# Query and gate projections a token chunk ahead of their cross-attention, with the second set held in an input buffer

## The chip, the cores and the metric

The program runs on one core of one Trainium2 chip. The metric is the device time of one execution in microseconds (us). A core has TensorE (PE in the profile, its weight loads PEld), VectorE (DVE), ScalarE (ACT), GpSimd (POOL) and SyncE (SP), which issues nearly all transfers here. Each engine works through its own list of instructions in a fixed order and stops at an instruction whose semaphores are not yet up.

## The reference, cut to what matters

```python
h = rmsnorm(x, pre_norm_w[i])                 # 4096 tokens x 1024
u = h @ w_in[i]
y_ssm  = mamba2_group(u[..., :SSM_IN], ...)                    # 512 columns
y_rwkv = rwkv7_group(u[..., SSM_IN:SSM_IN + RWKV_IN], ...)     # 256 columns
y_mem  = memory_xattn_group(u[..., SSM_IN + RWKV_IN:], mem_k, mem_v)   # 256 columns
y = jnp.concatenate([y_ssm, y_rwkv, y_mem], axis=-1)
x = x + rmsnorm(y @ w_out[i], post_norm_w[i])

def memory_xattn_group(u, mem_k, mem_v):      # 4 heads x 64, 256 memory tokens
    q = u[..., :XATTN_WIDTH].reshape(b, l, XATTN_HEADS, HEAD_DIM)
    g = u[..., XATTN_WIDTH:]
    s = jnp.einsum('blhd,bmhd->bhlm', q, mem_k) * (HEAD_DIM ** -0.5)
    p = jax.nn.softmax(s, axis=-1)
    o = jnp.einsum('bhlm,bmhd->blhd', p, mem_v).reshape(b, l, XATTN_WIDTH)
    return o * jax.nn.silu(g)
```

## The kernel before

The 4096 tokens are worked in 16 chunks of 256. Three phases follow one another: a (Mamba), b (RWKV) and c (cross-attention, output projection, norm and residual). The change touches phase c alone, which begins near 1587 us, while the last RWKV chunks are still being finished. Every float32 operand of a product is split into a high and a low part (`hh`/`hl`, `yh`/`ylo`, `phi`/`plo`, `wo0h`/`wo0l`), and a product is three matmuls: high by high, high by low, low by high.

For chunk i phase c has these streams:

- `load_hT(i)` (L112) fetches the normalised, transposed input of the chunk, `hh` and `hl`, 1 MB each, in two DMAs on SP. There are two buffers for it.
- `qg` (L1067) makes queries and gate. The 48 matmuls of `proj_cm` (L137, 128x256) for the queries go into one PSUM tile `pq`, the 48 for the gate into another, `pg`; both are `ps_pj` tiles, of which there are two in turn. `qs` is then split off `pq` by ACT and DVE (L1077, L1078), and the gate `sg` made by a tanh on ACT (L1084) and a product on DVE (L1085) that reads `pg` last.
- `units` does the four heads, named by a pair p and a side g: `score(p, g)` is 4 matmuls (L1110, L1111) into the PSUM tile `ps_g` or `ps_yo`, then a maximum (L1112), an exponential with its sum (L1115) and the division (L1119); `turn(p, g)` is 4 transposes (L1128) into `ps_tr` and their split into `phi` (ACT) and `plo` (DVE, L1132); `values(p)` is 8 matmuls (L1140) into a `ps_pj` tile, combined, gated and split into rows 6 and 7 of `yh`/`ylo`.
- `rest` loads the other rows of Y, which phases a and b have written (L1093).
- `outp(i)` (L1160) projects the two halves t=0 and t=1 of the chunk: 24 matmuls (L147, 128x512) into `ps_yd` and 24 into `ps_st`. Then the norm: ACT squares and sums both (L1172), POOL makes the factor in three small steps (L1174 to L1176), DVE scales both halves out of PSUM (`ot`, L1179), POOL adds the residual (L1180), SP stores (L1181). The next half's first `ps_yd` matmul waits for the first L1179, because there is one tile of each.

The loop at the end of phase c runs, for each i, `outp(i-1)`, `attn(i)` (that is `qg`, `rest`, `units`) and `load_hT(i+1)` beside one another. `weave` (L95) merges such streams by the weights written beside them, which fixes the order in which the instructions are written; a scheduler then fixes one list per engine. The transition is `start` (L1199): chunk 0's `qg`, memory keys and values, the load of chunk 1, the conversion of the first half of `w_out`, all woven with the end of the RWKV chain (`tail`; its steps on PE are L878, L885, L895, L912, L915, L946). The second half of `w_out` (`wo1`) is loaded later, through the two `xr` buffers (L1239).

Of the kernel before, what the change touches and what calls it, by code (L numbers as in the profile page):

```python
# [14 lines left out]
P = 128  # L15
# [12 lines left out]
def tile_hymba_trunk(  # L28
# [123 lines left out]
    def chain(*gens):  # L152
        for gen in gens:
            yield from gen
# [864 lines left out]
    def phase_c(b_tail, b_l, wqg, r14):  # L1019
# [41 lines left out]

        def attn(i, hT, Y):
            r = ahead if i == 1 else {}
            if i > 1:
                yield from qg(hT, r, 24)
            rest(i, Y)
            yield from units(Y, r)  # L1067

        def qg(hT, r, step):
            qs = [ca.tile([P, 2, NT], F32R, name=f"qs{h}", tag=f"qs{h}") for h in range(2)]  # L1070
            pq = ps_pj()
            for b_ in range(2):
                yield from proj_cm(blocks(wq)[b_], hT, pq[:, b_ * NT:(b_ + 1) * NT], step)
            pqv = pq.rearrange("p (b t) -> p b t", b=2)
            for h in range(2):
                hs, os_ = slice(h * 64, h * 64 + 64), slice((1 - h) * 64, (1 - h) * 64 + 64)
                s.copy(out=qs[h][hs], in_=pqv[hs])  # L1077
                v.tensor_tensor(out=qs[h][os_], in0=pqv[hs], in1=qs[h][hs].bitcast(F32), op=ALU.subtract)  # L1078
            pg = ps_pj()
            for b_ in range(2):  # L1080
                yield from proj_cm(blocks(wxg)[b_], hT, pg[:, b_ * NT:(b_ + 1) * NT], step)
            pgv = pg.rearrange("p (b t) -> p b t", b=2)
            sg = ca.tile([P, 2, NT], F32, name="sg", tag="sg")
            s.activation(out=sg, in_=pgv, func=AF.Tanh, scale=0.5)  # L1084
            v.scalar_tensor_tensor(out=sg, in0=sg, scalar=1.0, in1=pgv, op0=ALU.add, op1=ALU.mult)  # L1085
            r.update(qs=qs, sg=sg)

# [9 lines left out]
        def units(Y, r, tags=("g", "yo")):  # L1097
# [53 lines left out]

            for step in ((score, 0, 0), 1, (score, 0, 1), 1, (score, 1, 0), 3, (turn, 0, 0), 1, (turn, 0, 1), 4, (values, 0), 1,
                         (score, 1, 1), 1, (turn, 1, 0), 5, (turn, 1, 1), 4, (values, 1), 1):
                if isinstance(step, tuple):
                    step[0](*step[1:])
                else:
                    for _ in range(step):
                        yield

        def outp(i, Y):  # L1160
            for t in range(NPT):
                j = i * NPT + t
                xr = cw.tile([P, D], F32, name="xr", tag="xr", bufs=2)
                sy.dma_start(out=xr, in_=x2[j * P:(j + 1) * P, :])
                pos = [psum("yd", 1), psum("st", 1)]
                for n_ in range(2):
# [29 lines left out]
        late = ExitStack()  # L1196
        ahead = {}

        def start():  # L1199
            hT = new_hT()  # L1200
            yield from load_hT(0, hT)
            r = {}
            with right("cm") as cm:
                yield from chain2(memory(cm), qg(hT, r, 8))
            wr = ctx.enter_context(right("wr"))
            ws = late.enter_context(right("ws"))
            hT1 = new_hT()
            yield from load_hT(1, hT1)
            both = [units(Ys[0], r, None), chain(*(load_o(wr, ws, n_) for n_ in range(2)))]
            while both:  # L1210
                for gen in list(both):
                    if next(gen, gen) is gen:
                        both.remove(gen)
                    yield
            yield from qg(hT1, ahead, 8)
            rest(0, Ys[0], range(2))
# [30 lines left out]
        Ys.append(new_Y(cw))  # L1247
        hT = None
        for i in range(1, NS + 1):
# [3 lines left out]
            if i < NS:  # L1253
                streams.append((attn(i, hT, Ys[i % 2]), 28))
            if i + 1 < NS:
                hT = new_hT()
                streams.append((load_hT(i + 1, hT), 4))
            weave(*streams)
# [31 lines left out]
```

## Time and profile before

| what | value |
|---|---|
| time, median of 3 runs | 2271.78 us (2269.9 to 2273.0) |
| the profiled execution | 2275.23 us, its span 2273.5 us |
| granted TensorE clock over the span | 0.98 of full speed |
| PE busy | 2179.0 us (96%) |
| DVE, ACT, POOL busy | 1521.4, 1182.1, 709.0 us |
| DMA | 218.87 MB, mean 96 GB/s |

The span runs from the first to the last instruction on the core. PE busy counts overlapped matmuls once; a matmul's shown duration is longer than the distance to the next one, since they are pipelined. "Idle before <- X" names what ended an engine's wait.

### The profile page before, as it was taken

What the parts mean: (1) busy time and instruction counts of PE and PEld (TensorE: products, weight loads), DVE (VectorE), ACT (ScalarE), POOL (GpSimd) and SP (SyncE); (2) the same over time, 40 slices, a digit from 0 to 9 for tenths busy, and PEclk for the clock granted to TensorE, in tenths of its full rate; (3) what the DMA queues carried; (4) which work ended last, traced back from release to release, by engine and by line L of the source; (5) the groups of instructions that cost most, each with busy time, mean ns of one, the idle gap of its engine ahead of it and who ended that gap; (6) DMA issues with size and microseconds to landing.
All of it is one profiled execution on the core that took longest, in us unless ns stands there. A gap on an engine that the chain in (4) does not pass through costs nothing.

```text
span 2273.5 us, 51147 instructions
## 1 busy us (share of the span) xinstructions
PE 2179.0 (96%) x20705; PEld 1997.3 (88%) x20705; DVE 1521.4 (67%) x3442; ACT 1182.1 (52%) x2877; POOL 709.0 (31%) x1039
## 2 busy tenths in 40 slices
PE   4999999999999889999999999999899999999997
PEld 4999999999999788898989889888778888888885
DVE  5788878877878877667677777776644544545442
ACT  6555555545554565566666666676533433334331
POOL 1343434343433343333343333331122221222212
PEclk8999999999999999999999999998899999999999
DMA  6232223322233321111111111124333333333321
GB/s 200 88 139 91 94 94 113 121 94 94 93 139 105 116 83 39 67 57 48 43 44 63 61 48 44 44 90 163 121 135 130 125 121 144 113 115 125 121 70 56
DMA packets 83611, 218.87 MB, mean 96 GB/s; under 512 B 9191, under 2 KB 45486, under 8 KB 71086
## 3 DMA queue, kind: packets, MB, share of 16 engines
q1 hardware_dynamic: 82334, 215.59, 27.2%
q8 instruction: 163, 2.67, 0.5%
q14 instruction: 74, 0.61, 0.1%
q10 hardware_dynamic: 1040, 0.00, 0.0%
HBM read 152.00 MB, written 63.57 MB: 95 GB/s over the span
## 4 chain that ended last, share of the span: by engine, by line
PE 78%; DVE 8%; ACT 5%; DMA 4%; POOL 2%; issue 2%; POOLq 0%; SPq 0%; DVEq 0%; ACTq 0%
PE ps_pj L137 37%; PE ps_yd L147 8%; PE ps_pj L147 7%; PE ps_st L147 7%; DVE cc L296 3%; DMA R<-rowd 1%; PE ps_yo L878 1%; DMA w_st<-in_w_in_dram 1%; PE ps_yd L730 1%; PE ps_yd L425 1%; PE ps_tr L126 1%; ACT w_hi L78 1%; PE ps_yo L895 1%; PE ps_yo L885 1%; PE ps_st L730 1%
## 5 line engine op out<-in xcount | busy, mean ns | idle before, releaser
L137 PE MATMUL ps_pj<-hh,w_hi 128*128 128x256 f32 x2704 | 789.4, 292 | 7.2 <-ACT w_hi L78 5.4
L137 PE MATMUL ps_pj<-hh,w_lo 128*128 128x256 f32 x2704 | 778.6, 288 | 1.5 <-DVE w_lo L79 1.5
L137 PE MATMUL ps_pj<-hl,w_hi 128*128 128x256 f32 x2704 | 776.8, 287 | 0.0
L137 PEld LDWEIGHTS ps_pj<-hh,w_hi 128*128 128x128 f32 x2704 | 519.4, 192 | 18.8 <-issue 4.0
L137 PEld LDWEIGHTS ps_pj<-hh,w_lo 128*128 128x128 f32 x2704 | 519.1, 192 | 8.1 <-DVE w_lo L79 2.5
L137 PEld LDWEIGHTS ps_pj<-hl,w_hi 128*128 128x128 f32 x2704 | 519.7, 192 | 6.8
L296 DVE SCALAR_TENSOR_TENSOR cc<-ux,cwh,cc 128x256 f32<-128x256 f32 x384 | 220.0, 615 | 16.0 <-ACT cc L293 12.4
L147 PE MATMUL ps_pj<-w_hi,hh 128*128 128x260 f32 (+1 forms) x528 | 156.5, 297 | 22.4 <-DVE dtr L270 16.8
L147 PE MATMUL ps_pj<-w_hi,hl 128*128 128x260 f32 (+1 forms) x528 | 153.1, 290 | 0.0
L147 PE MATMUL ps_pj<-w_lo,hh 128*128 128x260 f32 (+1 forms) x528 | 152.5, 289 | 0.0
L147 PEld LDWEIGHTS ps_pj<-w_hi,hh 128*128 128x128 f32 x528 | 102.5, 194 | 25.1 <-issue 16.9
L147 PE MATMUL ps_yd<-wo0h,yh 128*128 128x512 f32 x256 | 103.9, 406 | 12.0 <-DVE ot L1179 12.0
L147 PE MATMUL ps_st<-wo1h,yh 128*128 128x512 f32 x256 | 103.8, 406 | 0.0
L147 PEld LDWEIGHTS ps_pj<-w_lo,hh 128*128 128x128 f32 x528 | 102.5, 194 | 0.3
L147 PEld LDWEIGHTS ps_pj<-w_hi,hl 128*128 128x128 f32 x528 | 102.4, 194 | 0.0
L147 PE MATMUL ps_yd<-wo0l,yh 128*128 128x512 f32 x256 | 102.3, 400 | 0.0
L147 PE MATMUL ps_yd<-wo0h,ylo 128*128 128x512 f32 x256 | 101.9, 398 | 0.0
L147 PE MATMUL ps_st<-wo1l,yh 128*128 128x512 f32 x256 | 101.7, 397 | 0.0
L147 PE MATMUL ps_st<-wo1h,ylo 128*128 128x512 f32 x256 | 100.8, 394 | 0.0
L299 ACT ACTIVATE th<-cc 128x512 f32<-128x512 f32 x64 | 40.4, 632 | 112.0 <-DVE cc L296 110.5
L1113 POOL TENSOR_SCALAR mx<-mx 128x2 f32<-128x2 f32 x64 | 14.6, 228 | 260.3 <-DVE mx L1112 238.1
L1180 POOL TENSOR_TENSOR xr<-ot,xr 128x512 f32<-128x512 f32 x64 | 84.7, 1347 | 32.7 <-DVE ot L1179 32.7
(443 smaller groups left out, 5086.0 us busy)
## 6 DMA issues: line engine op xcount, KB each, us to landing
hl<-hTd SPq DMA_DIRECT2D x32, 1024.0 KB
hh<-hTd SPq DMA_DIRECT2D x32, 1024.0 KB
xt<-in_x_dram SPq DMA_DIRECT2D x32, 512.0 KB
hTd<-hh SPq DMA_DIRECT2D x16, 1024.0 KB
hTd<-hl SPq DMA_DIRECT2D x16, 1024.0 KB
R<-rowd SPq DMA_DIRECT2D x32, 512.0 KB
xr<-in_x_dram SPq DMA_DIRECT2D x32, 512.0 KB
out_dram<-xr SPq DMA_DIRECT2D x32, 512.0 KB
```

The costliest lines, as they stand in the source:

```text
L78: s.activation(out=hi[:, ki, :], in_=st[:, k, 0:n], func=AF.Copy, scale=sc)
L126: te.transpose(pt[:, q * P:(q + 1) * P], src[:, k * P:(k + 1) * P], ident)
L137: te.matmul(outp, lhsT=a[:, k, :], rhs=b[:, k, :], start=(n == 0), stop=(n == 3 * KB - 1))
L147: te.matmul(outp, lhsT=a[:, k, tsl], rhs=b[:, k, 0:ncol], start=(n == 0), stop=(n == 3 * KB - 1))
L296: v.scalar_tensor_tensor(out=cc[:, b_, :], in0=ux[:, b_, j:j + NT], scalar=wj(j), in1=cc[:, b_, :], op0=ALU.mult, op1=ALU.add)
L299: s.activation(out=th, in_=cc, func=AF.Tanh)
L425: te.matmul(yd[hf * 64:hf * 64 + 64, h * 64:h * 64 + 64], lhsT=R[:, h, hf * 64:hf * 64 + 64], rhs=xdt[:, h * 64:h * 64 + 64], start=True, ...
L730: te.matmul(pa[:, c_ * P:(c_ + 1) * P], lhsT=BK[hs, p_, c_].rearrange("p a t -> p (a t)"), rhs=AR[hs, p_, c_].rearrange("p a t -> p (a t)" ...
L878: te.matmul(pch[hs, p_ * C:p_ * C + C], lhsT=AT[:, pc, h, 0:C], rhs=UV[:, pc, h, :], start=True, stop=True)
L885: te.matmul(pch[hs, 128 + p_ * C:128 + p_ * C + C], lhsT=TT[hs, pc].rearrange("p a t -> p (a t)"), rhs=X[hs, p_, :], start=True, stop=True)
L895: te.matmul(pch[hs, 256 + p_ * C:256 + p_ * C + C], lhsT=BKt[:, pc, hs], rhs=UV[:, pc, h, :], start=True, stop=True)
L1180: g.tensor_tensor(out=xr[:, cs], in0=ots[n_], in1=xr[:, cs], op=ALU.add)
```

## The change

Queries and gate get two lasting sets of buffers, used by even and odd chunks. The first is allocated outright; the second takes the place of one of the two input buffers: `qs` lies in its `hh`, `sg` in its `hl`. So one input buffer is left, and the load for chunk i+2 follows the projections of chunk i+1, which are its last readers. `qg` leaves `attn`: beside `outp(i-1)` and `attn(i)` there now runs `qg(i+1)` and behind it `load_hT(i+2)`. In `start`, `qg` of chunk 1 is woven beside chunk 0's heads. The order of the heads in `units` is another, and `outp` of the last chunk's first half uses the PSUM tiles `ps_g` and `ps_yo`, which scores no longer need there. The number of matmuls, of elementwise instructions and of bytes moved stays as it was. Lines below the edit lie 3 further down (L1079 to L1092 a little less or more).

```diff
-        def attn(i, hT, Y):
-            r = ahead if i == 1 else {}
-            if i > 1:
-                yield from qg(hT, r, 24)
+        def attn(i, Y, r):
             rest(i, Y)
             yield from units(Y, r)
...
+        qsets = [{"qs": [ca.tile([P, 2, NT], F32R, name=f"qs{h}") for h in range(2)], "sg": ca.tile([P, 2, NT], F32, name="sg")}]
+
+        def second_set():
+            a_ = new_hT()
+            qsets.append({"qs": [a_[0][:, h * 2:h * 2 + 2, :] for h in range(2)], "sg": a_[1][:, 0:2, :].bitcast(F32)})
...
         def qg(hT, r, step):
-            qs = [ca.tile([P, 2, NT], F32R, name=f"qs{h}", tag=f"qs{h}") for h in range(2)]
+            qs = r["qs"]
...
-            for step in ((score, 0, 0), 1, (score, 0, 1), 1, (score, 1, 0), 3, (turn, 0, 0), 1, (turn, 0, 1), 4, (values, 0), 1,
-                         (score, 1, 1), 1, (turn, 1, 0), 5, (turn, 1, 1), 4, (values, 1), 1):
+            for step in ((score, 0, 0), 1, (score, 0, 1), 5, (turn, 0, 0), (score, 1, 0), 1, (turn, 0, 1), (score, 1, 1), 4,
+                         (values, 0), 2, (turn, 1, 0), 1, (turn, 1, 1), 4, (values, 1), 1):
...
-                pos = [psum("yd", 1), psum("st", 1)]
+                pos = [psum("g", 1), psum("yo", 1)] if j == 2 * NS - 2 else [psum("yd", 1), psum("st", 1)]
...
-            hT1 = new_hT()
-            yield from load_hT(1, hT1)
-            both = [units(Ys[0], r, None), chain(*(load_o(wr, ws, n_) for n_ in range(2)))]
+            hTc.append(new_hT())
+            yield from load_hT(1, hTc[0])
+            second_set()
+            both = [units(Ys[0], qsets[0], None), chain(*(load_o(wr, ws, n_) for n_ in range(2))), qg(hTc[0], qsets[1], 8)]
...
-            yield from qg(hT1, ahead, 8)
+            yield from load_hT(2, hTc[0])
...
             if i < NS:
-                streams.append((attn(i, hT, Ys[i % 2]), 28))
+                streams.append((attn(i, Ys[i % 2], qsets[i % 2]), 26))
             if i + 1 < NS:
-                hT = new_hT()
-                streams.append((load_hT(i + 1, hT), 4))
+                ahead = [qg(hTc[0], qsets[(i + 1) % 2], 8)]
+                if i + 2 < NS:
+                    ahead.append(load_hT(i + 2, hTc[0]))
+                streams.append((chain(*ahead), 20))
             weave(*streams)
```

**First place: PE beside the output projection of a middle chunk.** Before, this stands ahead of the second half's first `ps_yd` matmul (L1128 are transposes, L1140 the values; `DVE_49` and the like are semaphores):

```order
L1140 MATMUL ps_pj<-phi,vm 128x256 [waits Activation_49]
L1128 MATMUL ps_tr<-ident,pr 128x128 [waits DVE_49,PE_49]
L1128 MATMUL ps_tr<-ident,pr 128x128 [waits DVE_49]
L1128 MATMUL ps_tr<-ident,pr 128x128 x2
L1140 MATMUL ps_pj<-plo,vm 128x256 [waits DVE_49]
L1140 MATMUL ps_pj<-phi,vm 128x256
L1140 MATMUL ps_pj<-plo,vm 128x256
L1140 MATMUL ps_pj<-phi,vm 128x256 [waits Activation_49]
L147 MATMUL ps_yd<-wo0h,yh 128x512 [waits DVE_49]
L147 MATMUL ps_yd<-wo0l,yh 128x512
```

In the changed kernel the place of the second half reads (L137 is the gate's projection for the next chunk, L1113 a score, L1143 the values of the second pair):

```order
L137 MATMUL ps_pj<-hh,w_lo 128x256
L1113 MATMUL ps_g<-kh_21597,qs_21602 128x256
L1114 MATMUL ps_g<-kl_21599,qs_21602 128x256
...
L1113 MATMUL ps_yo<-kh_21598,qs_21603 128x256 [waits Activation_49]
L1114 MATMUL ps_yo<-kl_21600,qs_21603 128x256
L1143 MATMUL ps_pj<-phi,vm 128x256 [waits DVE_49,Activation_49]
L1113 MATMUL ps_yo<-kh_21598,qs_21603 128x256
L1114 MATMUL ps_yo<-kl_21600,qs_21603 128x256
L147 MATMUL ps_yd<-wo0h,yh 128x512 [waits DVE_49]
L147 MATMUL ps_yd<-wo0l,yh 128x512
```

Between the last `ps_st` matmul of the first half and this place there now stand 24 matmuls of the gate, 8 transposes, 4 and 2 matmuls of scores; and one matmul of `values(1)` stands ahead of `ps_yd`, with a wait for DVE. Its `ps_pj` tile is the one that `pg` of the next chunk held.

**The same place on DVE.** Before, the gate's product stands directly behind the split of the queries:

```order
L1078 TENSOR_TENSOR qs_24895<-ps_pj,qs_24895 64x512 [waits Activation_49]
L1078 TENSOR_TENSOR qs_24896<-ps_pj,qs_24896 64x512 [waits Activation_49]
L1085 SCALAR_TENSOR_TENSOR sg<-sg,ps_pj 128x512 [waits Activation_49]
L1112 TENSOR_REDUCE mx<-ps_g 128x2 [waits PE_49]
L1112 TENSOR_REDUCE mx<-ps_yo 128x2 [waits PE_49]
```

In the changed kernel it stands behind the evacuation of the output projection (L1182 scales, L1135 and L1153 split, L1115 is a maximum; `hl` is the second set's `sg`):

```order
L1151 TENSOR_TENSOR ya<-ya,sg 128x256 [waits DVE_49]
L1182 SCALAR_TENSOR_TENSOR ot<-ps_yd,sq,pnw 128x512 [waits Pool_49]
L1182 SCALAR_TENSOR_TENSOR ot<-ps_st,sq,pnw 128x512
L1135 TENSOR_TENSOR plo<-ps_tr,phi 128x512 [waits Activation_49]
L1153 TENSOR_TENSOR ylo<-ya,yh 128x256 [waits Activation_49]
L1115 TENSOR_REDUCE mx<-ps_g 128x2 [waits PE_49]
L1089 SCALAR_TENSOR_TENSOR hl<-hl,ps_pj 128x512 [waits Activation_49]
L1135 TENSOR_TENSOR plo<-ps_tr,phi 128x512 [waits DVE_49]
```

So four instructions stand between the first L1182 and the product L1089. PE and DVE stand like this in the ten chunks 6 to 15, and the earlier ones nearly so.

**Second place: PE at the transition from the RWKV chain.** Before, a step of the chain (L878) is followed by scores of chunk 0 (L1110) and the next step (L885):

```order
L878 MATMUL ps_yo<-UV,AT 64x64 [waits Activation_49] x2
L878 MATMUL ps_yo<-UV,AT 64x64 x2
L1110 MATMUL ps_pj<-kh_21598,qs_21755 128x256 [waits DVE_49,PE_49]
L1111 MATMUL ps_pj<-kl_21600,qs_21755 128x256
...
L1110 MATMUL ps_pj<-kh_21597,qs_21754 128x256 [waits Activation_49]
...
L885 MATMUL ps_yo<-X,TT 64x64 [waits Activation_49]
```

In the changed kernel 35 matmuls of `qg` of chunk 1 stand first, and the rest of it goes on behind L885:

```order
L878 MATMUL ps_yo<-UV,AT 64x64 [waits Activation_49] x2
L878 MATMUL ps_yo<-UV,AT 64x64 x2
L137 MATMUL ps_pj<-hh,w_hi 128x256 [waits DMAHW3_49,DVE_49,PE_49]
L137 MATMUL ps_pj<-hl,w_hi 128x256 [waits DMAHW2_49]
L137 MATMUL ps_pj<-hh,w_lo 128x256
...
L1113 MATMUL ps_pj<-kh_21598,qs_21603 128x256 [waits Activation_49]
L1114 MATMUL ps_pj<-kl_21600,qs_21603 128x256
...
L885 MATMUL ps_yo<-X,TT 64x64 [waits Activation_49]
```

All of `qg` of chunks 1, 2 and 3 now stands ahead of the first `ps_st` matmul of `outp(0)`; before it was `qg` of chunk 1 and most of chunk 2's.

**Third place: the end on PE.** Before, the last matmuls of chunk 14's second half, a few values, the last chunk's first half, and directly behind it the second half:

```order
L147 MATMUL ps_st<-wo1h,ylo 128x512
L1140 MATMUL ps_pj<-phi,vm 128x256 [waits Activation_49]
L1140 MATMUL ps_pj<-plo,vm 128x256 [waits DVE_49]
L1140 MATMUL ps_pj<-phi,vm 128x256
L1140 MATMUL ps_pj<-plo,vm 128x256
L147 MATMUL ps_yd<-wo0h,yh 128x512 [waits DVE_49]
...
L147 MATMUL ps_st<-wo1h,ylo 128x512
L147 MATMUL ps_yd<-wo0h,yh 128x512 [waits DVE_49]
L147 MATMUL ps_yd<-wo0l,yh 128x512
```

In the changed kernel (L1143 are the last values of the last chunk, `ps_g` and `ps_yo` take its first half):

```order
L1143 MATMUL ps_pj<-phi,vm 128x256 [waits Activation_49]
L147 MATMUL ps_yd<-wo0h,yh 128x512 [waits DVE_49]
...
L147 MATMUL ps_st<-wo1h,ylo 128x512
L147 MATMUL ps_g<-wo0h,yh 128x512 [waits Activation_49]
...
L147 MATMUL ps_yo<-wo1h,ylo 128x512
L147 MATMUL ps_yd<-wo0h,yh 128x512 [waits DVE_49]
```

Between the last `ps_st` matmul of chunk 14's second half and the next `ps_yd` there are now 23 matmuls into `ps_g` and `ps_yo`; before there were 4 matmuls ahead of the first `ps_yd` shown and none ahead of the second.

## Rows read from the trace of the kernel before

**Rows 1.** Page, part 1: busy time, share of the span, instructions

```profile
PE 2179.0 (96%) x20705; PEld 1997.3 (88%) x20705; DVE 1521.4 (67%) x3442; ACT 1182.1 (52%) x2877; POOL 709.0 (31%) x1039
```

**Rows 2.** Windows: length, busy us and count per engine, granted clock (PEclk), DMA

```profile
1587.00:1606.00 19.00, 15.82 (x118) 12.33 (x118) 13.90 (x33) 13.50 (x40) 5.21 (x8) 0.64 0.40 147
1606.00:1624.00 18.00, 16.81 (x167) 15.33 (x165) 8.89 (x18) 7.79 (x19) 0.62 (x2) 1.00 0.26 77
1624.00:1645.00 21.00, 17.57 (x96) 14.52 (x94) 12.84 (x31) 10.12 (x29) 4.04 (x7) 0.84 0.46 163
1645.00:1682.00 37.00, 32.76 (x204) 29.04 (x203) 21.41 (x39) 17.11 (x42) 5.38 (x12) 1.00 0.57 191
1682.00:1701.00 19.00, 18.54 (x94) 15.87 (x95) 7.89 (x14) 3.79 (x11) 5.91 (x7) 0.91 0.16 55
1776.10:2181.70 405.60, 399.69 (x2401) 351.15 (x2401) 195.94 (x381) 146.69 (x402) 81.08 (x140) 1.00 0.34 119
2193.80:2264.70 70.90, 65.00 (x341) 54.54 (x339) 23.98 (x45) 17.59 (x51) 15.26 (x24) 0.98 0.15 55
```

**Rows 3.** Waits of PE, 1580 to 1701: us in total, times, longest

```profile
PE ps_pj L1140 <- ACT phi L1131: 4.7, 4, 3.2
PE ps_pj L1140 <- DVE plo L1132: 2.7, 3, 1.3
```

**Rows 4.** Waits of PE, 1776.1 to 2181.7

```profile
PE ps_yd L147 <- DVE ot L1179: 5.4, 11, 0.5
```

**Rows 5.** Waits of PE, 2193.8 to 2265

```profile
PE ps_yd L147 <- DVE ot L1179: 5.7, 3, 2.8
```

**Rows 6.** Chain that ended last, 2168 to 2200: start, us, what

```profile
2171.74 4.13 PE ps_st L147 x18
...
2188.91 0.44 PE ps_tr L1128 x4
...
2194.80 4.79 PE ps_pj L137 x40
```

**Rows 7.** Timeline 2248 to 2257, all engines: start, us, what, [idle before]

```profile
2248.53 0.39 PE L147 MATMUL ps_st<-wo1h,ylo 128*128 128x512 f32 x1
2249.01 0.60 ACT L1172 ACTIVATE ot<-ps_st 128x512 f32<-128x512 f32 x1 [4.32 <-PE ps_st L147]
...
2249.78 0.19 POOL L1174 TENSOR_TENSOR sq<-sq 128x1 f32<-128x1 f32 x1 [9.43 <-ACT ot L1172]
...
2250.91 0.75 DVE L1179 SCALAR_TENSOR_TENSOR ot<-ps_yd,sq,pnw 128x512 f32<-128x512 f32 x1 [10.28 <-POOL sq L1176]
2251.58 0.74 DVE L1179 SCALAR_TENSOR_TENSOR ot<-ps_st,sq,pnw 128x512 f32<-128x512 f32 x1
...
2251.72 0.50 PE L147 MATMUL ps_yd<-wo0h,yh 128*128 128x512 f32 x1 [2.80 <-DVE ot L1179]
...
2253.64 0.63 PE L147 MATMUL ps_yd<-wo0l,yh 128*128 128x512 f32 x1
...
2256.62 0.39 PE L147 MATMUL ps_yd<-wo0h,ylo 128*128 128x512 f32 x1
```

**Rows 8.** Groups of DVE, 1776.1 to 2181.7: count | busy, mean ns | idle before

```profile
L1132 DVE TENSOR_TENSOR plo<-ps_tr,phi 128x512 fp32r<-128x512 f32 x40 | 27.5, 687 | 38.0 <-ACT phi L1131 38.0
...
L1085 DVE SCALAR_TENSOR_TENSOR sg<-sg,ps_pj 128x512 f32<-128x512 f32 x10 | 6.9, 687 | 51.3 <-ACT sg L1084 51.3
```

**Rows 9.** Timeline of DVE, 2023.5 to 2024.6

```profile
2023.84 0.42 DVE L1150 TENSOR_TENSOR ylo<-ya,yh 128x256 fp32r<-128x256 f32 x1 [0.47 <-ACT yh L1149]
```

**Rows 10.** Timeline of DVE, 2037.4 to 2039

```profile
2037.64 0.97 DVE L1150 TENSOR_TENSOR ylo<-ya,yh 128x256 fp32r<-128x256 f32 x1 [0.48 <-ACT yh L1149]
```

**Rows 11.** Timeline of SP, 1880 to 1886

```profile
1884.05 0.32 SPq L113 DMA_DIRECT2D hl<-hTd  x1
```

**Rows 12.** Windows, 1884 to 1898 (last two columns: DMA share, GB/s)

```profile
1884.00:1891.20 7.20, 7.20 (x38) 6.02 (x37) 3.45 (x9) 3.22 (x11) 0.44 (x2) 1.00 0.75 291
1891.20:1898.00 6.80, 6.21 (x40) 5.14 (x39) 4.32 (x9) 4.29 (x13) 1.48 (x6) 1.00 0.00 0
```

## What the change should do to the time: the prediction

> **What bounds the kernel now.** I read the page first: PE is busy for 96% of the span [rows 1], so the kernel is bound by TensorE, the amount of whose work the change leaves alone. What it can win or lose is PE's idle time and the time at the lower clock. So next I cut phase c, the only part that the change touches, into windows [rows 2] and read three stretches apart.
>
> The transition, 1587 to 1701, is 114 us, of which PE is busy for 15.8 + 16.8 + 17.6 + 32.8 + 18.5 = 101.5: 12.5 us are idle. The reader should also see the clock: 0.64, 0.84 and 0.91 in three of the windows, where full speed (2.4 GHz) is 1.00 and the lower level (1.2 GHz) 0.5. A mean of 0.64 over 19 us is 13.7 us at the lower level; the other two give 6.7 and 3.4, together 23.8 us at half speed. Were PE busy throughout them, half of this, 11.9 us, would be lost; since idle time lies among them I count 8. So some 20 us are lost here. The list of PE's waits names the splits of the softmax weights (7.4 us of the idle, one wait of 3.2) [rows 3]; the rest is small waits between the RWKV steps.
>
> The middle, 1776 to 2182, is 405.6 us and holds ten chunks (the gate's product stands there 10 times [rows 8]): 40.56 us each, at full clock. The work of one chunk is worked out from the chain's pitches [rows 6]: a 128x256 matmul 4.79/40 = 0.12, a 128x512 one 4.13/18 = 0.23, a transpose 0.11. With 96 of `qg` (11.5), 96 of the output projection (22.1), 32 of scores and values (3.8) and 16 transposes (1.8) that is 39.2. So 1.3 us of each chunk are lost; 0.5 of it is the wait of the second half's `ps_yd` for DVE's evacuation of the first [rows 4], the rest lies in shorter ones just ahead of it.
>
> The end, 2194 to 2265: three waits for the same evacuation make 5.7 us, the longest 2.8 [rows 5]. Behind that longest one the rows are 0.63 long and 0.43 apart (2253.64 to 2256.62, 7 steps) where they are otherwise 0.39 long and 0.23 apart [rows 7]: the engine that idled for 2.8 us drops soon after to the lower clock, which costs some 8 x 0.2 = 1.6 us (the window's clock, 0.98 of 70.9, says 1.4) [rows 2]. In all 7.3.
>
> **The change part by part.** *The transition.* `qg` of chunk 1 now fills the RWKV chain's gaps and all three of chunks 1 to 3 stand ahead of the first `ps_st` of `outp(0)`, where before only one and most of the second stood. If the first `ps_st` starts when it did (it waits for `wo1`, whose loads go through SP behind the same RWKV store, so it cannot be much earlier), one `qg`, 11.5 us, is work that no longer has to follow: a gain of 11.5. It can be more, as far as 16, if the filled gaps also keep the clock up; the 20 us lost are the ceiling. It can be less: L878 and L885 are steps of one chain, and 35 matmuls now stand between them, 4.2 us at full and 8.4 at half clock, where 8 scores stood. The loads for chunks 2 and 3 use the one input buffer, and each can start only when the `qg` before it is done; one such load took 7 us (below). Two of these stalls would leave 3. I take 11.
>
> *The middle.* Gone is the lost 1.3, but for starts of a few hundredths: 1.2. The evacuation is hidden with room: from the issue of the last `ps_st` matmul (2248.53 + 0.23) the undisturbed chain takes ACT at 2249.01, POOL at 2249.78, DVE at 2250.91, and PE goes on at 2251.72, 2.96 us after [rows 7]. In the new order 24 matmuls of the gate (2.9), 8 transposes (0.9) and 6 scores (0.7), 4.5 us, stand in that place. But behind them stands one matmul of `values(1)` whose PSUM tile was `pg`'s, so it waits for the gate's product on DVE (L1089), and that stands behind both `ot`, a `plo`, a `ylo` and a maximum. From the same zero: first `ot` at 2.15; the second 0.67 later (2250.91 to 2251.58) [rows 7]; then, at about 0.63 from start to start, `plo` at 3.45 and `ylo` at 4.1; then the maximum, whose score is there by 4.4, and the product at 5.0 to 5.6, which takes 0.69 [rows 8]: done at 5.7 to 6.3, seen by PE 0.15 later. The bounds come from `ylo`, which takes 0.42 alone [rows 9] and 0.97 where POOL's residual add runs beside it [rows 10]; here that add does run, since it follows the first `ot`. The stall is 5.85 − 4.5 = 1.35 to 6.45 − 4.5 = 1.95; I take 1.7, nearer to the disturbed row. Queued behind the waiting matmul are all of `ps_yd` of the second half and `values(1)`, so nothing can slip past it: PE loses it in full. Each chunk: −1.2 + 1.7 = +0.5, eleven of them +5.5 (from +0.15 to +0.9 each: 2 to 10).
>
> Rows 9 and 10 are the same instruction and differ by 0.55 us. The Trainium skill (SBUF — State Buffer, section Who interferes with whom) says that a VectorE instruction with two SBUF inputs and a GpSimd instruction that reads SBUF hold a shared port pair exclusively, so that the loser waits; this trace agrees. By it all the `ylo` in that place would be of the long kind and the stall 1.95, the sum 2.8 us higher than mine.
>
> *The end.* 23 matmuls into `ps_g` and `ps_yo`, 5.3 us by the 0.23 pitch, now lie over each evacuation of 2.96, so the long waits go, and with them the half-clock stretch; some starts remain. Of 7.3 I take 6.5 (bounds 5 and 7.3).
>
> *At no cost:* the splits of `qs` into the second set are the same instructions on other addresses; the new order of heads is in the count above. The input load: its first DMA was issued at 1884.05 and the transfers were over by 1891.2 [rows 11, 12], 7.2 us for 2 MB. Between the last reader of the one buffer (the last gate matmul) and the next `qg` stand 16 matmuls of scores and values (1.9) and 48 of the output projection (11.0), 12.9 us in all. It is hidden by 5.7.
>
> **The sum.** −11 + 5.5 − 6.5 = −12. The profiled execution took 2275.2, so it becomes 2263.2; it lies 3.4 us above the median of the runs, so the median goes from 2271.8 to 2259.8.
>
> **The rivals.**
> - *The transition isn't shortened* (the chain L878 to L885 is what ends last, and 35 matmuls in its gap delay it): for it speaks that the chain's windows show PE idle and DVE and ACT busy for two thirds of the first one [rows 2]. −1 + 5.5 − 6.5 = −2 to −6: 2266 to 2270, say 2268. Chance 0.16.
> - *More is won*: the transition gives 16 and the stall in the middle is near its lower bound: −16 + 2 − 7 = −21, 2251. For it speaks the ceiling of 20 lost there. 0.14.
> - *The clock falls behind each of the new waits.* Now a wait of 0.5 leaves the clock at 1.00 [rows 2, 4], one of 2.8 drops it [rows 7]; 1.7 lies between. If it falls in each chunk at the price shown at the end, 1.6, eleven chunks cost 17 more: 2277. The Trainium skill (TensorE: Matmul & The Clock Gate, section HAM oscillation — how this bites in real kernels) describes a wait that recurs in each pass of a loop and brings the lower clock each time. Against it: of three waits at the end of together 5.7, the window's clock leaves room for one such stretch [rows 2, 5]. Where it happens in some chunks it ends at 2268 to 2277. 0.13.
> - *On the other side: the load of the one input buffer comes late.* It must be issued, moved and seen between the last gate matmul and the next `qg`, 12.9 us. The price is zero up to there and then the excess, in each of 12 chunks: at 14.5 us it is +1.6 x 12 = 19, 2279; at 15, 2285. For it speaks that SP issues in order and that loads of Y and of `xr` and the store lie beside it; against it the 7.2 us measured at 291 GB/s, with nothing in the next 6.8 us [rows 12]. 0.09.
> - My own forecast, 2255 to 2264: 0.48.
>
> **How the numbers follow.** About 0.2%, 4.5 us, is what a measurement of this kernel can tell from no change: 2267.3 to 2276.3 is "same". Faster: 0.48 + 0.14, and of the first rival 0.07 and a little of the third, 0.02: 0.71. Same: 0.09 of the first rival, 0.06 of the third and 0.01 of the load: 0.16. Slower: 0.05 of the third, 0.08 of the load: 0.13. The range 2248 to 2275 holds the forecast, the better case, the first rival and half of the clock's; it leaves out some 0.19: the tail of the better case (0.04), the other half of the clock's (0.06) and the late load (0.09). The forecast's own range is 2255 to 2264.
>
> **What would show it.** Right: PE's windows in the transition at 6 us of idle or less, with a clock above 0.8 in each; a period of 41 us in the middle with one wait of 1.3 to 2 of a values matmul (L1143) on DVE's gate product (L1089), and none of `ps_yd` on `ot`; at the end no wait over 1 us and the clock at 1.00. Wrong: the wait on `sg` missing (then the middle gains 10 us instead of losing 5), a period with a clock under 0.98, a wait of the first `qg` matmul on a load of `hh` or `hl` in each chunk, or RWKV steps further apart than before.

## The result and the profile after

The changed kernel takes 2232.57 us (median of 4 runs, 2229.08 to 2233.7) beside 2270.84 us before (4 runs, 2269.86 to 2273.0): ratio 0.9835, 95% interval 0.9823 to 0.9847, 38 us faster. The forecast was 12 us faster, in a range of 2248 to 2275; the time lies below it.

The profiled execution has a span of 2230.1 us instead of 2273.5, 43.4 less. Not all of it is the change's: up to the RWKV chain's step L878 both kernels run the same list of matmuls on PE, and that step stands 4.6 us earlier in the one trace than in the other. Timeline of PE, before:

```profile
1585.80 0.76 PE L878 MATMUL ps_yo<-UV,AT 128*64 128x64 f32 x8 [0.63 <-ACT UV L871]
```

and in the changed kernel:

```profile
1581.19 0.77 PE L878 MATMUL ps_yo<-UV,AT 128*64 128x64 f32 x8 [0.63 <-ACT UV L871]
```

So 38.8 us were won behind it, in phase c. The windows of the changed kernel that answer to [rows 2] (the transition in four windows, eight chunks of the middle, the end):

```profile
1582.40:1607.00 24.60, 24.07 (x223) 22.34 (x225) 17.27 (x40) 16.20 (x48) 5.06 (x9) 0.93 0.34 109
1607.00:1617.00 10.00, 7.09 (x64) 6.03 (x65) 5.38 (x12) 3.70 (x10) 0.40 (x1) 0.66 0.49 180
1617.00:1652.00 35.00, 33.42 (x257) 29.91 (x254) 22.16 (x50) 17.37 (x47) 5.71 (x11) 1.00 0.37 123
1652.00:1693.00 41.00, 40.60 (x260) 36.52 (x259) 27.77 (x53) 19.93 (x51) 8.59 (x14) 1.00 0.46 169
1845.80:2159.00 313.20, 313.20 (x1923) 280.04 (x1922) 150.48 (x305) 119.08 (x320) 68.40 (x113) 1.00 0.37 128
2159.00:2220.80 61.80, 61.20 (x289) 50.40 (x287) 22.83 (x45) 17.36 (x50) 16.47 (x25) 1.00 0.25 90
```

The reader should see three things. In the transition PE idles 0.5 + 2.9 + 1.6 + 0.4 = 5.4 us instead of 12.5, and the clock is low in one window of 10 us (0.66) and briefly in another. In the middle PE is busy for the whole 313.2 us: 39.15 us a chunk, which is the 39.2 that the prediction worked out as the work of a chunk, where it was 40.56. At the end the clock stays at 1.00 and 0.6 us are idle. PE's waits from 1700 to the end are a single one, where [rows 4, 5] had fourteen:

```profile
PE ps_pj L1143 <- DVE plo L1135: 0.6, 1, 0.6
```

To compare kernels by stretches of equal work I sum, over PE's matmuls behind L878, the distance from each start to the next less the pitch of its kind (0.119, 0.231 and 0.11 us, as in [rows 6]). Of the RWKV chain's small matmuls, several of which start close together, only what a distance has above some 0.1 us is counted. What is left is lost to idle time, to the lower clock and to the start of a matmul behind a wait. The transition is the first 100 us of work, the middle the next 450, the end the rest. A loss of −1 means that the pitches are a little too large. Each row is one profiled execution, in us:

```
kernel                      transition  middle    end   all
before                            29.8    14.4   10.2  54.4
changed                           16.5    -1.1    1.1  16.5
changed, on another chip          16.0    -1.2    1.2  16.0
values share the gate's tile      16.1    -0.9    1.3  16.5
old order of heads                15.9     0.8    1.6  18.3
no other tiles at the end         15.6    -1.2   11.1  25.5
no early projection of 1          21.9    -1.2    1.3  22.0
load made twice                   24.7     6.4    1.0  32.1
ahead, but in one line            18.4     6.8    2.4  27.6
split load of chunk 2             15.8    -1.1    1.1  15.8
start written earlier             17.3    -1.1    1.1  17.3
before + other tiles              27.0    14.6    1.2  42.8
before + new order of heads       27.5    16.8   12.3  56.6
```

54.4 − 16.5 = 37.9 agrees with the 38 us between the medians, and within 1 us with the 38.8 of the two traces, which count every distance in full: 13.3 in the transition, 15.5 in the middle, 9.1 at the end. The time of phases a and b, which no kernel here changes, differs from one execution to another by up to 10 us (L878 stands between 1576 and 1586 in these traces), so this table separates what the times alone leave unclear. One row is not quite of the same work: where the start is written earlier, 60 matmuls of phase c stand ahead of that L878.

### The profile page after: what moved, and what is told of

It is laid out like the page before. It is cut to its first block, busy times and chain, and to the rows that moved or that the text cites. A ratio compares the mean times of both kernels' runs of the same rounds, so it can differ in the third digit from the quotient of the medians.

```text
span 2230.1 us, 51100 instructions
## 1 busy us (share of the span) xinstructions
PE 2159.6 (97%) x20705; PEld 1990.6 (89%) x20705; DVE 1511.5 (68%) x3442; ACT 1184.1 (53%) x2877; POOL 714.6 (32%) x1039
## 4 chain that ended last, share of the span: by engine, by line
PE 84%; DVE 6%; DMA 4%; ACT 3%; issue 1%; POOL 1%; SPq 0%; POOLq 0%; ACTq 0%; DVEq 0%
PE ps_pj L137 39%; PE ps_pj L147 8%; PE ps_yd L147 8%; PE ps_st L147 8%; DVE cc L296 2%; PE ps_yd L425 1%; PE ps_yo L878 1%; PE ps_pj L1143 1%; PE ps_yd L730 1%; PE ps_tr L126 1%; DMA w_st<-in_w_in_dram 1%; PE ps_tr L1131 1%; DMA R<-rowd 1%; PE ps_yo L885 1%; PE ps_st L417 1%
## 5 line engine op out<-in xcount | busy, mean ns | idle before, releaser
L137 PE MATMUL ps_pj<-hh,w_hi 128*128 128x256 f32 x2704 | 791.0, 293 | 6.8 <-ACT w_hi L78 4.0
L137 PE MATMUL ps_pj<-hh,w_lo 128*128 128x256 f32 x2704 | 781.1, 289 | 2.2 <-DVE w_lo L79 2.1
L137 PE MATMUL ps_pj<-hl,w_hi 128*128 128x256 f32 x2704 | 778.9, 288 | 0.0
L137 PEld LDWEIGHTS ps_pj<-hh,w_hi 128*128 128x128 f32 x2704 | 520.5, 192 | 17.9 <-ACT w_hi L78 4.6
L137 PEld LDWEIGHTS ps_pj<-hh,w_lo 128*128 128x128 f32 x2704 | 520.2, 192 | 9.7 <-DVE w_lo L79 3.5
L137 PEld LDWEIGHTS ps_pj<-hl,w_hi 128*128 128x128 f32 x2704 | 521.0, 193 | 7.1
L147 PE MATMUL ps_pj<-w_hi,hh 128*128 128x260 f32 (+1 forms) x528 | 156.6, 297 | 21.3 <-DVE dtr L270 15.8
L1150 DVE TENSOR_TENSOR ya<-ps_pj,ya 64x256 f32<-64x256 f32 x64 | 26.9, 421 | 121.6 <-ACT ya L1149 121.3
L1183 POOL TENSOR_TENSOR xr<-ot,xr 128x512 f32<-128x512 f32 x64 | 89.3, 1418 | 42.4 <-DVE ot L1182 42.4
L1177 POOL TENSOR_TENSOR sq<-sq 128x1 f32<-128x1 f32 x32 | 6.4, 201 | 292.7 <-ACT ot L1175 292.7
L147 PE MATMUL ps_yd<-wo0h,yh 128*128 128x512 f32 x248 | 98.3, 396 | 0.0
L147 PE MATMUL ps_st<-wo1h,yh 128*128 128x512 f32 x248 | 97.5, 393 | 0.0
L147 PE MATMUL ps_yd<-wo0h,ylo 128*128 128x512 f32 x248 | 97.3, 392 | 0.0
L147 PE MATMUL ps_yd<-wo0l,yh 128*128 128x512 f32 x248 | 97.2, 392 | 0.0
```

Of the source, the lines that this page charges most:

```text
L137: te.matmul(outp, lhsT=a[:, k, :], rhs=b[:, k, :], start=(n == 0), stop=(n == 3 * KB - 1))
L147: te.matmul(outp, lhsT=a[:, k, tsl], rhs=b[:, k, 0:ncol], start=(n == 0), stop=(n == 3 * KB - 1))
L1150: v.tensor_tensor(out=ya[hs], in0=pg[hs], in1=ya[hs], op=ALU.add)
L1183: g.tensor_tensor(out=xr[:, cs], in0=ots[n_], in1=xr[:, cs], op=ALU.add)
```

## The experiments

**The changed kernel again**, beside others on one chip (no edit). 

> The changed kernel itself, beside the next two on one chip: 2229 to 2234, ratio to before 0.983 to 0.986.

Measured: 2231.39 us, ratio 0.9836 (0.9811 to 0.9861).

**The values in the gate's PSUM tile.** The step of the prediction that mattered most was a wait of `values(1)` for DVE's product on the gate.

```diff
             pgv = pg.rearrange("p (b t) -> p b t", b=2)
+            gate[:] = [pg]
...
-                po = ps_pj()
+                po = gate.pop() if p_ == 1 and gate else ps_pj()
```

> The changed kernel, with the second pair's values written into the very PSUM tile that the next chunk's gate projection held, as the prediction supposed. The step of the prediction: a wait of 1.35 to 1.95 us on the gate's product in each of eleven chunks, +15 to +21 on 2232.6, so 2248 to 2254. Rival: the scheduler sets the values behind the first output matmuls of the second half, where they wait for nothing, and the period stays at 39.1: 2231 to 2235.

Measured: 2232.91 us, ratio 0.9856 (0.9835 to 0.9876); the loss in the middle is −0.9. All eight matmuls of `values(1)` now stand behind the 24 of `ps_yd`, and the gate's product is long done when they come. PE, with the first `ps_yd` and the first of the values:

```profile
1884.99 0.40 PE L147 MATMUL ps_yd<-wo0h,yh 128*128 128x512 f32 x1
...
1890.45 0.28 PE L1145 MATMUL ps_pj<-phi,vm 128*128 128x256 f32 x1
```

and DVE's product on the gate:

```profile
1885.49 0.67 DVE L1091 SCALAR_TENSOR_TENSOR sg<-sg,ps_pj 128x512 f32<-128x512 f32 x1
```

Even with the tile that I supposed the wait would not have come about: nothing but the tile was changed, and the scheduler gave PE another list, with the values where they wait for nothing. The rival holds.

**The old order of heads in the changed kernel.**

```diff
-            for step in ((score, 0, 0), 1, (score, 0, 1), 5, (turn, 0, 0), (score, 1, 0), 1, (turn, 0, 1), (score, 1, 1), 4,
-                         (values, 0), 2, (turn, 1, 0), 1, (turn, 1, 1), 4, (values, 1), 1):
+            for step in ((score, 0, 0), 1, (score, 0, 1), 1, (score, 1, 0), 3, (turn, 0, 0), 1, (turn, 0, 1), 4, (values, 0), 1,
+                         (score, 1, 1), 1, (turn, 1, 0), 5, (turn, 1, 1), 4, (values, 1), 1):
```

> The changed kernel with the old order of heads. Theory of cover: a half of the output projection is slowed only if less than 2.96 us of other matmuls lie between the last of the half before and its first; here they are 4.4 and 5.6, as good as 4.8 and 5.2, so the middle stays at 39.1 a chunk and the time at 2232 to 2235. Rival: the order of heads is what removed the waits in the middle; then up to 1.4 us of each of eleven chunks come back, 2243 to 2248.

Measured: 2233.72 us, ratio 0.9858 (0.9838 to 0.9879), as the theory of cover has it. The new order is worth at most 2 us of loss, all in the middle and the end.

**The new order of heads alone, in the kernel before** (the edit of the change's loop over steps, nothing else). 

> The kernel before with only the new order of heads. Theory of cover: 2.4 us of other matmuls instead of 2.0 lie over the second half's evacuation, which needs 2.96; 0.4 us in each of eleven chunks: 3 to 6 us faster, ratio 0.997 to 0.999. Rival, that the order is what the gain in the middle came from: 1.4 us a chunk, 15 us, ratio 0.993.

Measured: 2265.82 beside 2266.57 us, ratio 0.9993 (0.9977 to 1.0008): no gain, where 3 to 6 us were expected. Cover alone did not forecast this. PE's waits in its middle (1760 to 2170):

```profile
PE ps_pj L1140 <- DVE plo L1132: 2.8, 10, 0.4
PE ps_yd L147 <- DVE ot L1179: 2.5, 10, 0.2
```

The wait for `ot` halves, from 0.5 to 0.2 a chunk, as 2.4 instead of 2.0 us of cover would have it; but in its place the values wait 0.3 for the split of the weights, since the order brings them sooner behind their transposes.

**Ahead, but not beside.** The projections stay one chunk ahead, in one line with the heads:

```diff
-            if i < NS:
-                streams.append((attn(i, Ys[i % 2], qsets[i % 2]), 26))
-            if i + 1 < NS:
-                ahead = [qg(hTc[0], qsets[(i + 1) % 2], 8)]
-                if i + 2 < NS:
-                    ahead.append(load_hT(i + 2, hTc[0]))
-                streams.append((chain(*ahead), 20))
+            work = [attn(i, Ys[i % 2], qsets[i % 2])] if i < NS else []
+            if i + 1 < NS:
+                work.insert(0, qg(hTc[0], qsets[(i + 1) % 2], 8))
+                if i + 2 < NS:
+                    work.insert(1, load_hT(i + 2, hTc[0]))
+            if work:
+                streams.append((chain(*work), 46))
```

> The changed kernel with the projections still one chunk ahead, but in one line with the heads (projections of chunk i+1, its next load, then the heads of chunk i) instead of a stream of their own beside them. If what the middle needed is an independent stream of matmuls between a head's steps: the second half's evacuation is covered by 2.5 us again and the values wait for their splits, 0.5 to 1.2 us a chunk, 6 to 13 more plus some 3 at the end, 2240 to 2248. If it is enough that the projections are a chunk ahead: 2231 to 2235.

Measured: 2245.27 us, ratio 0.9903 (0.9883 to 0.9923), against 2231.39 on the same chip. The middle loses 6.8 instead of −1.1, about half of what it lost before. (The profiled execution is the fastest of six, 2241.4, so the table shows 11.6 us of the 13.9 between the medians on this chip.) PE's waits from 1750 to 2150:

```profile
PE ps_yd L147 <- DVE ot L1182: 2.1, 10, 0.2
```

So being a chunk ahead gives one half of the gain in the middle, and the stream of its own beside the heads the other.

**The usual tiles at the end.** `pos` is `ps_yd` and `ps_st` for all halves. 

> The changed kernel with the last chunk's first half again in the usual two PSUM tiles. Theory: the waits at the end come back (two evacuations of 2.96 us that nothing covers, one covered by 1.5, and a stretch at the lower clock of 1.6): +8 to +9, 2240 to 2242. Rival: the end gained by the earlier query and gate projections alone: below 2235.

Measured: 2238.09 us, ratio 0.9879 (0.9858 to 0.99); less than the 2240 to 2242 expected, but the loss at the end goes from 1.1 to 11.1. From 2140 on PE has three waits for the evacuation again, as in [rows 5], and some of the values:

```profile
PE ps_yd L147 <- DVE ot L1182: 5.9, 3, 2.8
PE ps_pj L1143 <- DVE plo L1135: 0.9, 2, 0.6
PE ps_pj L1143 <- ACT phi L1134: 0.9, 1, 0.9
```

**The other tiles at the end alone, in the kernel before.** 

> The kernel before with only the other two PSUM tiles for the last chunk's first half. Theory of cover: two of the three long waits at the end go even without the early projections, since scores no longer need these tiles: 4 to 7 us faster than before, ratio 0.997 to 0.998. Rival: it needs the projections ahead and the other weave to bring anything: ratio 0.999 to 1.001.

Measured: 2259.21 beside 2266.57 us, ratio 0.996 (0.9947 to 0.9974). The loss at the end goes from 10.2 to 1.2, and of the three waits one is left (2150 to 2260):

```profile
PE ps_yd L147 <- DVE ot L1179: 0.5, 1, 0.5
```

This one line of the change is worth 9 to 10 us of the loss at the end, with or without the rest. By the medians it is 7.4 us in the kernel before and 5.5 in the changed one, where they are less sure than the loss, since phases a and b differ as said above.

**No early projection of chunk 1** in the transition:

```diff
-            both = [units(Ys[0], qsets[0], None), chain(*(load_o(wr, ws, n_) for n_ in range(2))), qg(hTc[0], qsets[1], 8)]
+            both = [units(Ys[0], qsets[0], None), chain(*(load_o(wr, ws, n_) for n_ in range(2)))]
...
+            yield from qg(hTc[0], qsets[1], 8)
             yield from load_hT(2, hTc[0])
```

> The changed kernel with chunk 1's projections behind chunk 0's heads in the transition again, not woven beside them. Theory: they are what fills the gaps of the RWKV chain; the loss in the transition goes from 16.6 back towards 29.9 us: +10 to +13, 2243 to 2246. Rival: the projections of chunks 2 and 3, which are ahead in this kernel too, fill as much: 2232 to 2236.

Measured: 2237.93 us, ratio 0.9876 (0.9851 to 0.9901), between the two. Its windows in the transition:

```profile
1584.00:1608.00 24.00, 20.84 (x152) 17.51 (x153) 17.58 (x41) 16.43 (x47) 5.24 (x8) 0.64 0.24 77
1608.00:1620.00 12.00, 11.93 (x126) 10.85 (x124) 5.02 (x10) 3.93 (x10) 0.40 (x1) 1.00 0.27 81
1620.00:1645.00 25.00, 24.02 (x188) 22.48 (x188) 14.15 (x32) 11.75 (x30) 4.27 (x8) 1.00 0.50 176
```

The first 24 us look as they did before (clock 0.64, 3.2 us idle), so this is what chunk 1's projections fill: 5.4 us in the end. The other 7.9 of the 13.3 are still won, and in the third window: 1.0 us idle at full clock, where the kernel before idled 3.4 of 21 us at 0.84 [rows 2]. What stands there is all of chunk 2's projections, between the transposes and values of chunk 1, which before came by themselves. PE's groups of this kernel from 1628.5 to 1644:

```profile
L137 PE MATMUL ps_pj<-hh,w_lo 128*128 128x256 f32 x32 | 9.2, 288 | 0.0
L137 PE MATMUL ps_pj<-hl,w_hi 128*128 128x256 f32 x32 | 9.2, 288 | 0.0
L137 PE MATMUL ps_pj<-hh,w_hi 128*128 128x256 f32 x32 | 9.1, 285 | 0.0
L1131 PE MATMUL ps_tr<-ident,pr 128*128 128x128 f32 x16 | 2.5, 272 | 0.0
```

and those of the kernel before at the same place (1633 to 1644):

```profile
L1128 PE MATMUL ps_tr<-ident,pr 128*128 128x128 f32 x16 | 3.4, 350 | 0.7 <-ACT t L950 0.7
L1140 PE MATMUL ps_pj<-phi,vm 128*128 128x256 f32 x8 | 3.1, 386 | 0.9 <-ACT phi L1131 0.9
L1140 PE MATMUL ps_pj<-plo,vm 128*128 128x256 f32 x7 | 2.9, 427 | 1.6 <-DVE plo L1132 1.6
```

The same 16 transposes take 350 ns each there and 272 here: idle time and the lower clock both go when 96 independent matmuls stand between the steps.

**Each load of the input buffer made twice.**

```diff
-                    ahead.append(load_hT(i + 2, hTc[0]))
+                    ahead += [load_hT(i + 2, hTc[0]), load_hT(i + 2, hTc[0])]
```

> The changed kernel with each load of the one input buffer in the loop made twice, one behind the other (the same data; 4 MB instead of 2). The load is hidden: the trace of the changed kernel shows it issued at 1883.85 and read from 1896.71 on, 12.9 us, while the queue is at work on it until about 1891.5. Twice the bytes (7.5 us more) overrun this by some 3 us in each of twelve chunks: 2260 to 2275. If the time stays under 2240 the bytes of the load have far more room than thought; if it goes past 2290 the room was already used up.

Measured: 2245.28 us, ratio 0.9902 (0.9881 to 0.9923), less than forecast. 8.2 us are lost in the transition and 7.5 in the middle, where only 7 of the waits from 1700 to 2160 are seen:

```profile
PE ps_pj L137 <- DMA hh<-hTd: 5.1, 7, 1.4
```

SP's timeline of one such place, and the first projection that reads the load: the second pair goes out 5.1 and 8.4 us behind the first, the last DMA at 1944.22, 7.5 us before the projection starts.

```profile
1935.41 0.32 SPq L113 DMA_DIRECT2D hl<-hTd  x1
1935.83 0.38 SPq L113 DMA_DIRECT2D hh<-hTd  x1
...
1940.55 0.32 SPq L113 DMA_DIRECT2D hl<-hTd  x1
1944.22 0.32 SPq L113 DMA_DIRECT2D hh<-hTd  x1
1951.70 0.36 PE L137 MATMUL ps_pj<-hh,w_hi 128*128 128x256 f32 x1 [1.43 <-DMA hh<-hTd]
```

The DMA engines are busy the whole time between, in the second window also with rows of Y and `xr` (windows, last two columns the DMA share and GB/s):

```profile
1935.40:1944.00 8.60, 8.60 (x47) 7.32 (x47) 5.24 (x13) 3.82 (x13) 2.44 (x4) 1.00 0.88 292
1944.00:1951.70 7.70, 6.27 (x36) 5.30 (x35) 3.51 (x7) 3.43 (x10) 1.34 (x5) 1.00 1.02 418
```

From the first issue to the projection it is 16.3 us, of which PE waited 1.4, so twice the bytes just miss a room of 14.9 us. It is not the 12.9 that I had taken over from the changed kernel: the list of this run has 8 score matmuls and 8 transposes more between the last gate matmul and the next `qg`. That is why the overrun is smaller than forecast; the load itself took, in this place, no less than the 15 us that I had reckoned with. In the changed kernel the single load is issued at 1883.85 and first read at 1896.71, and the share of the DMA engines falls from 0.94 in the microsecond from 1891 to 0.49 and 0.26 in the next two: some 4 us are to spare, PE waits for no load from 1700 on, and the one input buffer costs nothing in the middle.

**Chunk 2's load in four pieces, and the start written earlier.** In the transition PE still idles 2.9 us from 1607 to 1617 while chunk 2's load is on its way. The waits that make up the 2.9 us are the RWKV chain's own (changed kernel, waits of PE from 1575 to 1700):

```profile
PE ps_yo L895 <- ACT UV L890: 2.0, 1, 2.0
PE ps_yd L912 <- DVE ST L898: 0.5, 1, 0.5
PE ps_yo L885 <- ACT X L881: 0.4, 1, 0.4
```

Whether chunk 2's projections could fill them if the load came earlier is what the two edits ask. The first edit loads by halves of the contraction:

```diff
-            yield from load_hT(2, hTc[0])
+            for ks in (slice(0, 4), slice(4, 8)):
+                for n_ in range(2):
+                    sy.dma_start(out=hTc[0][n_][:, ks, :].bitcast(F32), in_=hTd[2][:, n_, ks])
+                yield
```

> The changed kernel with chunk 2's input load in four DMAs by halves of the contraction instead of two, so that the first projections need only half of the bytes. The changed kernel's PE idles near 1608 to 1612 of its trace and has the lower clock to 1617, while this load is on its way. If the load is what is missing there: 2 to 5 us faster than the changed kernel, 2228 to 2231. If the RWKV chain is: the same, 2231 to 2234.

Measured: 2229.51 us, ratio 0.9834 (0.9812 to 0.9855). The time lies where the load was to be what is missing, but the ratio is that of the changed kernel itself (0.9835 and 0.9836), and the loss in the transition is 15.8 instead of 16.0 to 16.5, so the 2 to 3 us by which this time is lower are not shown to come from the edit. The second adds a larger weight for `start` in the weave (80 instead of 52). 

> The changed kernel with the split load of chunk 2 and with the transition's stream written earlier beside the RWKV chain (weight 80 instead of 52). All that phase c still loses, some 16 us, lies in the transition. If the written order binds there: 3 to 8 us faster than the changed kernel, 2224 to 2229. If the RWKV chain and the loads do: within 2 us of it.

Measured: 2231.17 us, ratio 0.9842 (0.9818 to 0.9865), beside 2231.39 for the changed kernel: the same. Neither cutting up the load nor the weight wins any of the last 16 us that can be told apart. What would is not shown.

## Why the prediction was wrong

**What bounds the kernel: right.** The 39.2 us worked out for a chunk from the pitches is what a chunk now takes (39.15). The losses counted from the windows, 20 in the transition, 1.3 in each of eleven chunks and 7.3 at the end, are 42 us; the table has 54.4, most of the difference in the transition (29.8), and 37.9 of them went.

**The transition: right in size, partly by luck.** −11 forecast, −13.3 measured. That chunk 1's projections fill the chain's gaps is shown by taking them away (5.4 us); that the rest comes from chunk 2's is read from the groups above and not tried by itself. The mechanism named was partly another: I had argued from one projection less to follow, on the condition that the first `ps_st` starts when it did. It does not. Before:

```profile
1654.41 0.40 PE L147 MATMUL ps_st<-wo1h,yh 128*128 128x512 f32 x1
```

and in the changed kernel:

```profile
1658.53 0.40 PE L147 MATMUL ps_st<-wo1h,yh 128*128 128x512 f32 x1
```

That is 68.6 and 77.3 us behind the L878 shown above, 8.7 us later, while 127 matmuls of 128x256 and 12 transposes more stand ahead of it, 16.4 us by the pitches. So 7.7 us are won up to there and not 11.5, and the rest behind it; what went is idle time and low clock in two places, and that the sum came out near is luck in part. The 35 matmuls do delay the chain: its last L885 stands 36.3 us behind that L878 before (1622.08) and 38.6 in the changed kernel (1619.77), its last step, L946, 48.2 (1633.97) and 53.5 (1634.65). The gain came about in spite of these 5.3 us, so the first rival, by which the delay eats up the gain, does not hold.

**The middle: the step that failed.** It says: "behind them stands one matmul of `values(1)` whose PSUM tile was `pg`'s, so it waits for the gate's product on DVE (L1089)". I had dealt the two `ps_pj` tiles out in turn, in the order in which they are asked for: queries, gate, first values, second values. In the kernel before they do come in turn. In the changed program, in the chunks 3 to 14, both values take one tile, the one that held the queries, and the two banks change places from chunk to chunk:

```
PSUM bank of each ps_pj tile, in the order asked for; in the changed kernel queries and gate are the next chunk's
                                  queries  gate  first values  second values
before, chunks 1 to 15                  2     3             2              3
changed, chunks 1 and 2                 3     2             3              2
changed, chunks 3, 5, 7 to 13           3     2             3              3
changed, chunks 4, 6, 8 to 14           2     3             2              2
```

So `values(1)` waits there for the first values to be read (DVE's `ya`, L1150), not for the gate. (The sentence of the section on the change that its tile is the one that `pg` held is wrong for these chunks.) In chunks 1 and 2 it is the gate's tile, and PE's waits show none for the product there either. The times in the argument were good. PE at that place, with the last gate matmul, the values and the first `ps_yd`:

```profile
1883.66 0.28 PE L137 MATMUL ps_pj<-hh,w_lo 128*128 128x256 f32 x1
...
1884.49 0.28 PE L1143 MATMUL ps_pj<-phi,vm 128*128 128x256 f32 x1
...
1884.85 0.40 PE L147 MATMUL ps_yd<-wo0h,yh 128*128 128x512 f32 x1
```

and DVE:

```profile
1881.36 0.43 DVE L1150 TENSOR_TENSOR ya<-ps_pj,ya 64x256 f32<-64x256 f32 x1 [0.99 <-ACT ya L1149]
...
1882.28 0.75 DVE L1182 SCALAR_TENSOR_TENSOR ot<-ps_yd,sq,pnw 128x512 f32<-128x512 f32 x1
1882.95 0.74 DVE L1182 SCALAR_TENSOR_TENSOR ot<-ps_st,sq,pnw 128x512 f32<-128x512 f32 x1
...
1884.20 0.51 DVE L1153 TENSOR_TENSOR ylo<-ya,yh 128x256 fp32r<-128x256 f32 x1
...
1885.23 0.67 DVE L1089 SCALAR_TENSOR_TENSOR sg<-sg,ps_pj 128x512 f32<-128x512 f32 x1
```

The zero of the prediction's sum, the issue of the last `ps_st`, is 1879.82 + 0.23 = 1880.05 here. The first `ot` starts 2.23 behind it (forecast 2.15), the gate's product 5.18 (5.0 to 5.6), PE stands at the values 4.44 behind it (4.5). And the values' matmul starts 0.74 us before the product does, and 2.7 us after the `ya` that it does wait for has ended: there is no such wait. The prediction had named this sign itself, "the wait on `sg` missing". Of the term "−1.2 + 1.7 = +0.5, eleven of them +5.5" the first half was nearly right (−13 of −15.5) and the second was nothing: −15.5 measured, 21 us off, which is most of the error of 27. With the stall struck out the sum would have been −11 − 13 − 6.5 = −30.5. (Its upper bound has a slip: 1.95 − 1.2 is 0.75 a chunk and not 0.9, 8 us and not 10. Nothing hung on it.)

The Trainium skill's rule on the shared ports (SBUF — State Buffer, section Who interferes with whom) was weighed inside this term: a VectorE instruction with two SBUF inputs contends with a GpSimd instruction that reads SBUF. The trace agrees with the rule, but not with the length that I took from it. POOL's two adds follow one another there, the first from 1883.11 to 1884.43, and the `ylo` at 1884.20 ends at 1884.71, 0.28 us behind the end of the first. In all 25 places of both traces where a `ylo` starts while an add runs, it ends 0.28 us behind the end of that add. So it takes 0.97 where more than half a us of the add is left [rows 10] and 0.50 here in ten chunks, where 0.23 is left; with no add beside it, it takes 0.42 [rows 9]. Neither of the prediction's two lengths was the one of this place. No time hung on it.

**The end: right in kind, too small.** −6.5 forecast, −9.1 measured. The three waits and the stretch at the lower clock went, as forecast. The table's end begins some 20 us ahead of the window of [rows 5] and so holds 1.2 us of the chunk before, which the prediction counts with the middle; the rest are short waits of values ahead of the first of the three and the starts behind each wait, which I had not counted.

**The rivals.** The lower clock did not fall behind new waits, as there were none: 1.00 in the middle. The late load did not happen: issued at 1883.85, first read at 1896.71, and only a load of twice the size overruns. "More is won" was the right direction, at 2251 still 18 us short, since it kept a stall in the middle.

## What to carry to other kernels

A wait that is read off a list of instructions is only as good as the knowledge of which buffer stands behind the semaphore: look up the buffer that an instruction writes before pricing the wait, above all where a pool need not deal its buffers out in turn, as here. And a wait that is priced on one list may move when the list is made anew, as the run with the gate's tile shows. Where the matrix engine is the bound, add up its work per pass by the pitches first; the gap between that and the period is the most a reordering can give, and an independent stream of matmuls, a pass ahead and woven between the dependent steps, took all of it in the middle here. An evacuation at the end of a program, where no other work is left, may be covered by nothing more than other PSUM tiles for the last pass.

## What the runs showed of the hardware that I had not expected

The start of phase c, behind the same 16801 matmuls in twelve of the thirteen traces, lies between 1576 and 1586 us, so that two kernels' times of one execution each can differ by some 0.4% through a stretch that is the same in both. The granted clock fell in the transition of the changed kernel (0.66 over 1607 to 1617) at a wait of 2.0 us (L895 on ACT, over at 1610.77) among small matmuls of the RWKV chain and shorter waits. The second of the three waits of [rows 5] in the kernel before, 2.34 us up to 2237.57 behind a dense stream, left it at full speed: the rows behind it lie 0.23 us apart. So the length of the last wait alone does not tell.
